# Grouped-query attention: another PSUM split, another place for the division, and orders written out

## The chip, the cores and the metric

The kernel runs on one core of one Trainium2 chip. A core has a matrix engine (TensorE, PE in the profile), a vector engine (VectorE, DVE), an activation engine (ScalarE, ACT), a general engine (GpSimd, POOL), and SyncE (SP), which only issues transfers here. Each engine works through its own list of instructions in order and waits on semaphores for the others. Matmul results land in PSUM, eight banks of 2 KB per partition; everything else lives in SBUF. The metric is the device time of one execution in microseconds, lower is better.

## The reference

Eight batches, 512 positions, 32 query heads, 8 key/value heads, head size 64, all float32. Four query heads share a key/value head.

```python
scores = np.einsum('bhqd,bhkd->bhqk', Q, K_expanded) * scale      # scale = 1/sqrt(64)
weights = np.exp(scores - np.max(scores, axis=-1, keepdims=True))
weights = weights / (np.sum(weights, axis=-1, keepdims=True) + 1e-10)
output = np.einsum('bhqk,bhkd->bhqd', weights, V_expanded)
```

## The kernel before

The work is cut into 32 units: a batch and two neighbouring key/value heads, so 8 query heads. A unit has 4 pairs of query heads (`p` counts pairs, 128 in all, called slots below). A pair has 4 chunks of 128 keys (`kc`).

For one chunk `emit_scores_chunk` makes two matmuls (L169), one for each head `m`. Each uses 64 rows of the array (the head size), head 0 on partitions 0 to 63 and head 1 on 64 to 127, and writes 512 float32 columns, so the chunk's tile `s_unit` fills two PSUM banks with 128 keys by 2x512 queries. The exponential moves it to SBUF as bf16 (`pt`): three chunks in four by ScalarE's Exp (L186), the second one (`kc` = 1) by VectorE (L177), which computes bits of a bf16 number with one multiply and add. Nothing subtracts the maximum.

`emit_pv_chunk` multiplies `pt` by V (L206): 8 matmuls a chunk, 65 columns each, since V carries a column of ones that sums the weights. A pair's output is 8 blocks (2 heads by 4 query tiles `qc`) of 65 columns, and 4 matmuls, one a chunk, add up to a block: 128 of them a unit. `emit_norm` takes the reciprocal of the ones column (L223) and multiplies (L224) on VectorE, straight from PSUM, for each pair.

Q and K come in with positions on partitions, and PE turns them with `ident` (L118 for K, L130 for Q), 24 transposes a unit in three groups of 8, each copied out by VectorE (L120, L134). K is loaded twice into `k_nat`, so that each head's keys stand on both halves of the partitions.

PSUM: a ring of three two-bank tiles, `spsum_pool`, shared by scores and transposes, and one two-bank tile for the output (`pv_pool`). All loads and stores are issued by GpSimd, loads converting float32 to bf16: of a unit's eight loads six move rows of one head (64 numbers) and two, for Q, rows of 256, and a store moves rows of 512. The order of work on each engine is made by the framework's scheduler from the program's order.

Of the kernel before, what the change touches and what calls it, by code (L numbers as in the profile page):

```python
# [12 lines left out]
U16 = mybir.dt.uint16  # L14


@with_exitstack
def kernel(
# [7 lines left out]
    nc = tc.nc  # L26
# [7 lines left out]
    NPAIR = HPG // 2  # L34
    NSLOT = NU * 2 * NPAIR

    scale = 1.0 / math.sqrt(D)

    DVE_KC = 1

    SCHRAUD_C = 5.0
    LOAD_PREFETCH = 2
    STORE_DELAY = 2

    A_schr = (2.0 ** 7) / math.log(2.0) * scale
    B_schr = 127.0 * (2.0 ** 7) - SCHRAUD_C

    const_pool = ctx.enter_context(tc.tile_pool(name="const", bufs=1))
    qnat_pool = ctx.enter_context(tc.tile_pool(name="qnat", bufs=LOAD_PREFETCH + 2))
    knat_pool = ctx.enter_context(tc.tile_pool(name="knat", bufs=LOAD_PREFETCH + 2))  # L50
    v_pool = ctx.enter_context(tc.tile_pool(name="v", bufs=LOAD_PREFETCH + 2))
    qt_pool = ctx.enter_context(tc.tile_pool(name="qt", bufs=6))
    kt_pool = ctx.enter_context(tc.tile_pool(name="kt", bufs=3))
    pt_pool = ctx.enter_context(tc.tile_pool(name="pt", bufs=3))
    osb_pool = ctx.enter_context(tc.tile_pool(name="osb", bufs=STORE_DELAY + 2))
    misc_pool = ctx.enter_context(tc.tile_pool(name="misc", bufs=8))

    spsum_pool = ctx.enter_context(tc.tile_pool(name="spsum", bufs=3, space=bass.MemoryType.PSUM))
    pv_pool = ctx.enter_context(tc.tile_pool(name="pv", bufs=1, space=bass.MemoryType.PSUM))

    ident = const_pool.tile([128, 128], BF16)
    make_identity(nc, ident)

    def unit_bgp(u):
        return u // GP, u % GP

    loads = {}

    def emit_load_q(u):
        b, gp = unit_bgp(u)  # L70
        g0 = 2 * gp
        h_base = g0 * HPG
        q_nat = qnat_pool.tile([128, SC, 2, HPG, D], BF16, name="q_nat")
        for g in range(2):
            nc.gpsimd.dma_start(  # L75
                out=q_nat[:, :, g, :, :],
                in_=Q[b, :, h_base + g * HPG:h_base + (g + 1) * HPG, :].rearrange(
                    "(sc p) h d -> p sc h d", p=128
                ),
            )  # L80
        loads.setdefault(u, {})["q"] = q_nat

    def emit_load_k(u):
        b, gp = unit_bgp(u)
        g0 = 2 * gp
        k_nat = knat_pool.tile([128, SC, 2, 2, D], BF16, name="k_nat")
        for g in range(2):
            for c in range(2):
                nc.gpsimd.dma_start(  # L89
                    out=k_nat[:, :, g, c, :],  # L90
                    in_=K[b, :, g0 + g, :].rearrange("(sc p) d -> p sc d", p=128),
                )
        loads.setdefault(u, {})["k"] = k_nat

    def emit_load_v(u):
        b, gp = unit_bgp(u)
        g0 = 2 * gp
        v_tile = v_pool.tile([128, SC, 2, D + 1], BF16, name="v")
        nc.gpsimd.memset(v_tile[:, :, :, D:D + 1], 1.0)  # L99
        for g in range(2):  # L100
            nc.gpsimd.dma_start(  # L101
                out=v_tile[:, :, g, 0:D],
                in_=V[b, :, g0 + g, :].rearrange("(sc p) d -> p sc d", p=128),
            )
        loads.setdefault(u, {})["v"] = v_tile

    LOAD_BATCHES = (emit_load_q, emit_load_k, emit_load_v)

    trans = {}

    def emit_trans_kt(u):
        k_nat = loads[u]["k"]
        kt_ps = spsum_pool.tile([128, 2, S], FP32, name="s_unit")[:, 0, :].bitcast(
            BF16
        ).rearrange("p (g sc c) -> p g sc c", g=2, sc=SC)
        for g in range(2):
            for sc in range(SC):
                nc.tensor.transpose(kt_ps[:, g, sc, :], k_nat[:, sc, g, :, :], ident)  # L118
        kt_tile = kt_pool.tile([128, 2, S], BF16, name="kt")
        nc.vector.tensor_copy(out=kt_tile, in_=kt_ps)  # L120
        trans.setdefault(u, {})["kt"] = kt_tile

    def emit_trans_qt(u, g):
        q_nat = loads[u]["q"]
        qt_ps = spsum_pool.tile([128, 2, S], FP32, name="s_unit")[:, 0, :].bitcast(
            BF16
        ).rearrange("p (i sc c) -> p i sc c", i=NPAIR, sc=SC)
        for i in range(NPAIR):
            for sc in range(SC):
                nc.tensor.transpose(  # L130
                    qt_ps[:, i, sc, :], q_nat[:, sc, g, 2 * i:2 * i + 2, :], ident
                )
        qt_tile = qt_pool.tile([128, NPAIR, S], BF16, name="qt")
        nc.vector.tensor_copy(out=qt_tile, in_=qt_ps)  # L134
        trans.setdefault(u, {}).setdefault("qt", {})[g] = qt_tile

    TRANS_BATCHES = (
        emit_trans_kt,
        lambda u: emit_trans_qt(u, 0),
        lambda u: emit_trans_qt(u, 1),  # L140
    )

    pending_stores = {}

    def emit_store(u, split=False):
        b, gp = unit_bgp(u)
        h_base = 2 * gp * HPG
        o_sb = pending_stores.pop(u)
        nc.gpsimd.dma_start(  # L149
            out=out[b, :, h_base:h_base + 2 * HPG, :].rearrange(  # L150
                "(sc p) h d -> p sc h d", p=128
            ),
            in_=o_sb,
        )

    jobs = {}
    osb = {}

    def emit_scores_chunk(p, kc):
        st = jobs[p]  # L160
        u, g, i = st["u"], st["g"], st["i"]
        kt_all = trans[u]["kt"]
        qt_tile = trans[u]["qt"][g]
        pt_tile = st["pt"]
        pair_idx = st["pidx"]

        s_unit = spsum_pool.tile([128, 2, S], FP32, name="s_unit")
        for m in range(2):
            nc.tensor.matmul(  # L169
                s_unit[:, m, :],  # L170
                kt_all[64 * m:64 * m + 64, g, kc * 128:(kc + 1) * 128],
                qt_tile[64 * m:64 * m + 64, i, :],
                start=True,
                stop=True,
            )
        if kc == DVE_KC:
            nc.vector.tensor_scalar(  # L177
                out=pt_tile[:, kc, :, :].bitcast(U16),
                in0=s_unit[:, :, :],
                scalar1=float(A_schr),  # L180
                scalar2=float(B_schr),
                op0=mybir.AluOpType.mult,
                op1=mybir.AluOpType.add,
            )
        else:
            nc.scalar.activation(  # L186
                out=pt_tile[:, kc, :, :],
                in_=s_unit[:, :, :],
                func=mybir.ActivationFunctionType.Exp,
                scale=float(scale),  # L190
            )

    def emit_pv_chunk(p, kc):
        st = jobs[p]
        u, g = st["u"], st["g"]
        v_tile = loads[u]["v"]
        pt_tile = st["pt"]
        if kc == 0:
            pv_tile = pv_pool.tile([128, 2, 512], FP32, name="pv").rearrange(
                "p m (qc c) -> p m qc c", qc=SC  # L200
            )
            st["opsums"] = pv_tile[:, :, :, 0:D + 1]
        o_psums = st["opsums"]
        for qc in range(SC):
            for m in range(2):
                nc.tensor.matmul(  # L206
                    o_psums[:, m, qc, :],
                    pt_tile[:, kc, m, qc * 128:(qc + 1) * 128],
                    v_tile[:, kc, g, :],
                    start=(kc == 0 and qc == 0),  # L210
                    stop=(kc == SC - 1 and qc == SC - 1),
                )

    def emit_norm(p):
        st = jobs.pop(p)
        u, g, i = st["u"], st["g"], st["i"]
        if u not in osb:
            osb[u] = osb_pool.tile([128, SC, 2, NPAIR, 2, D], FP32, name="o_sb")
            pending_stores[u] = osb[u]
        o_sb = osb[u]  # L220
        o_psums = st["opsums"]
        inv = misc_pool.tile([128, 2, SC], FP32, name="inv")
        nc.vector.reciprocal(out=inv, in_=o_psums[:, :, :, D:D + 1])  # L223
        nc.vector.tensor_tensor(  # L224
            out=o_sb[:, :, g, i, :, :].rearrange("p qc m d -> p m qc d"),
            in0=o_psums[:, :, :, 0:D],
            in1=inv[:, :, :, None].to_broadcast((128, 2, SC, D)),
            op=mybir.AluOpType.mult,
        )
        if st["pidx"] == 2 * NPAIR - 1:  # L230
            osb.pop(u)
# [5 lines left out]
    for fn in TRANS_BATCHES:  # L237
        fn(0)
# [70 lines left out]
```

## Time and profile before

| what | value |
|---|---|
| median of 3 runs (lowest, highest) | 451.97 us (451.85, 452.49) |
| profiled execution, first to last instruction | 449.0 us |
| PE matmuls, busy | 371.9 us (83%) |
| VectorE, busy | 326.0 us (73%) |
| ScalarE, busy | 367.0 us (82%) |
| GpSimd, busy | 219.0 us (49%) |
| transfer engines, queue of GpSimd | 95.7% of 16 engines' span |
| bytes read from and written to memory | 58.72 MB, 33.55 MB |

The profile gives no time of its own for the profiled execution beside its span of 449.0 us; the median of the timed runs lies 3.0 us above that span. Busy time counts instructions from start to end, and matmuls overlap each other, so a busy PE can still take more. PEld is PE loading weights, one load ahead of every matmul. In rows of groups the number after the bar is the sum in us, then the mean in ns.

### The profile page before, as it was taken

To read this page: it belongs to the slowest core of one execution; us is meant where nothing else is said; L and a number is where in the kernel's file an instruction comes from. 1 tells how busy PE (TensorE), PEld (TensorE's weight loads), DVE (VectorE), ACT (ScalarE), POOL (GpSimd) and SP (SyncE) were. 2 spreads that over 40 slices of the span, in tenths; PEclk is the share of its full clock that TensorE was granted. 3 is DMA by queue.
4 is the path that set the end of the run, shared out by engine and by line. 5 is a ranking of instruction groups with operands and counts; after the bars stand their busy time and mean duration, and the time that the engine had idled before them with its cause. 6 is when DMAs were issued, how large, how long until landed. Compare 5 with 4: busy or idle time off the path is not lost.

```text
span 449.0 us, 13535 instructions
## 1 busy us (share of the span) xinstructions
PE 371.9 (83%) x5888; PEld 219.5 (49%) x5888; DVE 326.0 (73%) x480; ACT 367.0 (82%) x385; POOL 219.0 (49%) x326
## 2 busy tenths in 40 slices
PE   2888888888888888888888888888888888888882
PEld 1445545555455455455554554554545545545541
DVE  1577787777787777778777778777778777777761
ACT  1688888888888888888888888888888888888881
POOL 9988556454456554446645445645445652200000
PEclk9999999999999999999999999999999999999998
DMA  9999999999999999999999999999999999212222
GB/s 90 151 160 213 206 173 148 159 126 121 168 173 147 156 140 113 160 176 149 158 154 110 145 172 165 148 156 128 122 169 172 147 155 157 36 80 96 95 95 93
DMA packets 143930, 63.78 MB, mean 142 GB/s; under 512 B 102912, under 2 KB 135680, under 8 KB 143872
## 3 DMA queue, kind: packets, MB, share of 16 engines
q0 software_dynamic: 143872, 62.93, 95.7%
q8 instruction: 46, 0.75, 0.7%
q14 instruction: 12, 0.10, 0.1%
HBM read 58.72 MB, written 33.55 MB: 206 GB/s over the span
## 4 chain that ended last, share of the span: by engine, by line
PE 65%; issue 13%; ACT 11%; POOL 7%; DMA 1%; ACTq 1%; DVE 0%; POOLq 0%
PE s_unit L169 30%; PE pv L206 28%; ACT pt L186 11%; PE s_unit L130 5%; POOL k_nat L89 3%; PE s_unit L118 3%; POOL q_nat L75 2%; POOL v L101 1%; DMA q_nat<-in_Q_dram 1%; POOL out_dram L149 1%; ACTq L186 1%; DVE pt L177 0%; POOLq L304 0%; POOL v L99 0%; POOL ident masks.py:199 0%
## 5 line engine op out<-in xcount | busy, mean ns | idle before, releaser
L186 ACT ACTIVATE pt<-s_unit 128x1024 bf16<-128x1024 f32 x384 | 365.7, 1024 | 72.5 <-PE s_unit L169 72.5
L169 PE MATMUL s_unit<-qt,kt 64*128 64x512 bf16 x1024 | 191.0, 385 | 60.0 <-ACT pt L186 58.2
L206 PEld LDWEIGHTS <-pt 128*128 128x128 bf16 x4096 | 139.2, 98 | 114.9 <-issue 75.8
L206 PE MATMUL pv<-v,pt 128*128 128x65 bf16 x4096 | 170.3, 195 | 1.0 <-DVE o_sb L224 1.0
L177 DVE TENSOR_SCALAR pt<-s_unit 128x1024 uint16<-128x1024 f32 x128 | 156.3, 1221 | 16.1 <-PE s_unit L169 11.3
L89 POOL DMA_DIRECT2D k_nat<-in_K_dram x128 | 96.7, 783 | 1.2 <-issue 1.1
L224 DVE TENSOR_TENSOR o_sb<-pv,inv 128x512 f32<-128x512 f32 x128 | 88.5, 691 | 4.5
L169 PEld LDWEIGHTS <-kt 64*128 64x128 bf16 x1024 | 40.9, 94 | 97.1 <-issue 78.7
L223 DVE RECIPROCAL inv<-pv 128x8 f32<-128x8 f32 x128 | 26.6, 208 | 83.8 <-PE pv L206 83.8
L75 POOL DMA_DIRECT2D q_nat<-in_Q_dram x64 | 48.2, 766 | 47.1 <-PE s_unit L130 44.9
L99 POOL MEMSET v<- 128x8 bf16 x32 | 4.9, 152 | 122.6 <-PE pv L206 122.6
L101 POOL DMA_DIRECT2D v<-in_V_dram x64 | 47.9, 759 | 4.0 <-DMA q_nat<-in_Q_dram 0.7
L149 POOL DMA_DIRECT2D out_dram<-o_sb x32 | 24.9, 779 | 48.6 <-DVE o_sb L224 48.6
L134 DVE COPY qt<-s_unit 128x1024 bf16<-128x1024 bf16 x64 | 43.5, 679 | 2.4 <-PE s_unit L130 2.4
L130 PE MATMUL s_unit<-ident,q_nat 128*128 128x128 bf16 x512 | 39.9, 222 | 1.8 <-DMA q_nat<-in_Q_dram 1.7
L130 PEld LDWEIGHTS <-q_nat 128*128 128x128 bf16 x512 | 30.3, 99 | 2.4 <-DMA q_nat<-in_Q_dram 2.2
L120 DVE COPY kt<-s_unit 128x1024 bf16<-128x1024 bf16 x32 | 21.8, 680 | 9.5 <-PE s_unit L118 9.5
L118 PE MATMUL s_unit<-ident,k_nat 128*128 128x128 bf16 x256 | 20.5, 225 | 6.6 <-DMA k_nat<-in_K_dram 6.6
L118 PEld LDWEIGHTS <-k_nat 128*128 128x128 bf16 x256 | 15.4, 100 | 7.2 <-issue 5.7
L186 ACT ACT_TABLE_LOAD x1 | 1.3, 1283 | 0.7 <-PEq L293 0.7
masks.py:199 POOL TENSOR_SCALAR_AFFINE_SELECT ident<-ident 128x128 bf16<-128x128 bf16 x1 | 0.3, 305 | 0.1
masks.py:197 POOL MEMSET ident<- 128x128 bf16 x1 | 0.2, 205 | 0.3 <-POOLq L293 0.3
(4 smaller groups left out, 0.4 us busy)
## 6 DMA issues: line engine op xcount, KB each, us to landing
out_dram<-o_sb POOLq DMA_DIRECT2D x32, 1024.0 KB, 5.3
q_nat<-in_Q_dram POOLq DMA_DIRECT2D x64, 256.0 KB, 5.2
k_nat<-in_K_dram POOLq DMA_DIRECT2D x128, 64.0 KB, 4.9
v<-in_V_dram POOLq DMA_DIRECT2D x64, 64.0 KB, 3.1
```

The costliest lines, as they stand in the source:

```text
L75: nc.gpsimd.dma_start(out=q_nat[:, :, g, :, :], in_=Q[b, :, h_base + g * HPG:h_base + (g + 1) * HPG, :].rearrange("(sc p) h d -> p sc h d" ...
L89: nc.gpsimd.dma_start(out=k_nat[:, :, g, c, :], in_=K[b, :, g0 + g, :].rearrange("(sc p) d -> p sc d", p=128),)
L101: nc.gpsimd.dma_start(out=v_tile[:, :, g, 0:D], in_=V[b, :, g0 + g, :].rearrange("(sc p) d -> p sc d", p=128),)
L118: nc.tensor.transpose(kt_ps[:, g, sc, :], k_nat[:, sc, g, :, :], ident)
L130: nc.tensor.transpose(qt_ps[:, i, sc, :], q_nat[:, sc, g, 2 * i:2 * i + 2, :], ident)
L134: nc.vector.tensor_copy(out=qt_tile, in_=qt_ps)
L149: nc.gpsimd.dma_start(out=out[b, :, h_base:h_base + 2 * HPG, :].rearrange("(sc p) h d -> p sc h d", p=128), in_=o_sb,)
L169: nc.tensor.matmul(s_unit[:, m, :], kt_all[64 * m:64 * m + 64, g, kc * 128:(kc + 1) * 128], qt_tile[64 * m:64 * m + 64, i, :], start=True, ...
L177: nc.vector.tensor_scalar(out=pt_tile[:, kc, :, :].bitcast(U16), in0=s_unit[:, :, :], scalar1=float(A_schr), scalar2=float(B_schr), op0=my ...
L186: nc.scalar.activation(out=pt_tile[:, kc, :, :], in_=s_unit[:, :, :], func=mybir.ActivationFunctionType.Exp, scale=float(scale),)
L206: nc.tensor.matmul(o_psums[:, m, qc, :], pt_tile[:, kc, m, qc * 128:(qc + 1) * 128], v_tile[:, kc, g, :], start=(kc == 0 and qc == 0), sto ...
L224: nc.vector.tensor_tensor(out=o_sb[:, :, g, i, :, :].rearrange("p qc m d -> p m qc d"), in0=o_psums[:, :, :, 0:D], in1=inv[:, :, :, None]. ...
```

## The change

The units, the pairs, the chunks, the score matmuls and the split of the exponential between ScalarE and VectorE stay (the VectorE one has another additive constant). What differs:

- PSUM: a ring of three two-bank tiles for scores alone (`spsum`), and a ring of two one-bank tiles (`xpsum`) that transposes and outputs share.
- Outputs are made block by block: 4 matmuls in a row add up to one block. Blocks are gathered in groups of 7, 7, 7, 4 and 7 to a bank. VectorE copies a group as it is (`raw`), and once a unit takes the reciprocal of 32 sums (L212). GpSimd does the division for the whole unit (L214).
- K is turned once (4 transposes a unit, so 20 in all); two transfers on SyncE's queue make a copy with the halves exchanged (`kx`), and the head whose half is wrong reads that one.
- Loads: one for Q a unit, one for K and one for V a batch, rows of 512 numbers in all of them (1 KB in bf16). GpSimd spreads V to leave room for the ones column (`spread_v`).
- The order on all engines is the program's. After each chunk's scores a loop puts in filler (blocks of output, transposes) for 0.33 us by its own costs, if the next filler is ready by a lag of two chunks after its pair.

```diff
+    DVE_KC = 1
+    qn_pool = ctx.enter_context(tc.tile_pool(name="qn", bufs=PREF))   # PREF = 4
...
+    pt_pool = ctx.enter_context(tc.tile_pool(name="pt", bufs=4))
+    raw_pool = ctx.enter_context(tc.tile_pool(name="raw", bufs=3))
+    osb_pool = ctx.enter_context(tc.tile_pool(name="osb", bufs=3))
...
+    spsum = ctx.enter_context(tc.tile_pool(name="spsum", bufs=3, space=bass.MemoryType.PSUM))
+    xpsum = ctx.enter_context(tc.tile_pool(name="xpsum", bufs=2, space=bass.MemoryType.PSUM))
...
+    def load_q(u):
+        b, gp = divmod(u, GP)
+        t = qn_pool.tile([128, SC, HU * D], BF16, name="q_nat")
+        nc.gpsimd.dma_start(
+            out=t,
+            in_=Q[b, :, HU * gp:HU * (gp + 1), :].rearrange(
+                "(sc p) h d -> p sc (h d)", p=128
+            ),
+        )
...
+    def spread_v(b):
+        t = v1_pool.tile([128, SC, KV, D + 1], BF16, name="v1")
+        nc.gpsimd.memset(t[:, :, :, D:D + 1], 1.0)
+        nc.gpsimd.tensor_copy(
+            out=t[:, :, :, 0:D],
+            in_=vn.pop(b).rearrange("p sc (h d) -> p sc h d", h=KV),
+        )
...
             nc.tensor.matmul(
-                s_unit[:, m, :],
-                kt_all[64 * m:64 * m + 64, g, kc * 128:(kc + 1) * 128],
-                qt_tile[64 * m:64 * m + 64, i, :],
+                s[:, m, :],
+                kt[u][0 if m == g else 1][64 * m:64 * m + 64, kc * 128:(kc + 1) * 128],
+                qt[u][64 * m:64 * m + 64, i, :],
...
+    class Outputs:
...
+        def ready(self, step, lag):
+            pair = self.u * HPG + (self.first + self.at) // BLK
+            return step >= SC * (pair + 1) + lag
+        def emit(self):
...
+                self.o = xpsum.tile([128, 2048], mybir.dt.uint8, name="x").bitcast(FP32)
...
+            for kc in range(SC):
+                nc.tensor.matmul(
+                    self.o[:, self.at * (D + 1):(self.at + 1) * (D + 1)],
+                    pt[:, kc, m, qc * 128:(qc + 1) * 128],
+                    v1[u // GP][:, kc, 2 * (u % GP) + 2 * i // HPG, :],
+                    start=(self.at == 0 and kc == 0),
+                    stop=(self.at == self.n - 1 and kc == SC - 1),
+                    skip_group_check=True,
+                )
...
+            nc.vector.tensor_copy(
+                out=raws[u][:, self.first:self.first + self.n, :],
+                in_=self.o[:, 0:self.n * (D + 1)],
+            )
+            if self.first + self.n == HPG * BLK:
+                finish(u)
...
+    class Turn:
...
+            nc.tensor.transpose(self.x[:, self.at * 128:(self.at + 1) * 128], src, ident)
...
+                nc.vector.tensor_copy(out=k, in_=self.x[:, 0:S])
+                x = kt_pool.tile([128, S], BF16, name="kx")
+                nc.sync.dma_start(out=x[64:128], in_=k[0:64])
+                nc.sync.dma_start(out=x[0:64], in_=k[64:128])
...
+    def finish(u):
...
+        nc.vector.reciprocal(out=inv, in_=raw[:, :, D])
+        o = osb_pool.tile([128, SC, HU, D], FP32, name="o_sb")
+        nc.gpsimd.tensor_tensor(
+            out=o.rearrange("p qc h d -> p h qc d"),
...
+    COST = {Outputs: 0.122, Turn: 0.056}
+    QUOTA = 0.33
+    LAG = 2
+    def unit_fill(u):
+        yield Outputs(u, 0, 7)
+        yield Outputs(u, 7, 7)
+        if u + 2 < NU:
+            yield Turn(u + 2, 0)
+            yield Turn(u + 2, 1)
+        yield Outputs(u, 14, 7)
+        if u + 2 < NU:
+            yield Turn(u + 2, None)
+        yield Outputs(u, 21, 4)
+        yield Outputs(u, 25, 7)
+    with tc.manual_schedule(engines={PE, ACT, DVE, POOL, SP}):
+        load_k(0)
+        load_q(0)
+        load_q(1)
+        load_v(0)
+        load_q(2)
+        load_q(3)
+        spread_v(0)
+        for t in (Turn(0, None), Turn(0, 0)):
+            while not t.emit():
+                pass
+        fill = [Turn(0, 1), Turn(1, None), Turn(1, 0), Turn(1, 1)]
+        for u in range(NU):
+            fill.extend(unit_fill(u))
...
+                scores(p, kc)
+                budget += QUOTA
+                while budget > 0 and fill and fill[0].ready(step, LAG):
+                    f = fill[0]
+                    budget -= COST[type(f)]
+                    if f.emit():
+                        fill.pop(0)
...
+                budget = min(budget, 2 * QUOTA)
```

How the instructions stand now, at three places. On PE, in the middle of the kernel before, two chunks of scores stand together (tiles 2271 and 2275) between the last K transpose and the first output matmul of a run of 16:

```order
L118 MATMUL s_unit_2253<-ident_88,k_nat_1746 128x128
L169 LDWEIGHTS kt_2003
L169 MATMUL s_unit_2271<-qt_2074,kt_2003 128x512
L169 LDWEIGHTS kt_2003
L169 MATMUL s_unit_2271<-qt_2074,kt_2003 128x512
L169 LDWEIGHTS kt_2003
L169 MATMUL s_unit_2275<-qt_2074,kt_2003 128x512
L169 LDWEIGHTS kt_2003
L169 MATMUL s_unit_2275<-qt_2074,kt_2003 128x512
L206 LDWEIGHTS pt_2200
L206 MATMUL pv_2279<-v_1558,pt_2200 128x65
```

On PE in the changed kernel, around the K transposes of a unit (L189 is any transpose, L108 a score, L149 an output, `x` the one-bank tile):

```order
L189 LDWEIGHTS k_nat_101
L189 MATMUL x_611<-ident_94,k_nat_101 128x128
L108 LDWEIGHTS kt_372
L108 MATMUL s_616<-qt_301,kt_372 128x512
L108 LDWEIGHTS kx_374
L108 MATMUL s_616<-qt_301,kx_374 128x512
L189 LDWEIGHTS k_nat_101
L189 MATMUL x_611<-ident_94,k_nat_101 128x128
L149 LDWEIGHTS pt_495
L149 MATMUL x_626<-v1_113,pt_495 128x65
```

One chunk now stands alone between fillers. Over a unit in the steady part, PE's 16 chunks stand in 10 runs: 1, 2, 1, 3, 4 and five times 1 chunk, and the runs of 3 and 4 stand before and behind the longest filler, 32 output matmuls. Before, a unit had 8 runs of 2 chunks.

On VectorE before, for one unit (L120 and L134 copy transposes, L177 is its share of the exponential):

```order
L120 COPY kt<-s_unit 128x1024
L177 TENSOR_SCALAR pt<-s_unit 128x1024
L223 RECIPROCAL inv<-pv 128x8
L224 TENSOR_TENSOR o_sb<-pv,inv 128x2x4x64
L134 COPY qt<-s_unit 128x1024
L177 TENSOR_SCALAR pt<-s_unit 128x1024
L223 RECIPROCAL inv<-pv 128x8
L224 TENSOR_TENSOR o_sb<-pv,inv 128x2x4x64
```

VectorE now, one unit (L162 copies raw outputs):

```order
L117 TENSOR_SCALAR pt<-s 128x1024
L162 COPY raw<-x 128x455
L117 TENSOR_SCALAR pt<-s 128x1024
L162 COPY raw<-x 128x455
L203 COPY qt<-x 128x1024 x2
L117 TENSOR_SCALAR pt<-s 128x1024
L162 COPY raw<-x 128x455
L195 COPY kt<-x 128x512
L117 TENSOR_SCALAR pt<-s 128x1024
L162 COPY raw<-x 128x260
L162 COPY raw<-x 128x455
L212 RECIPROCAL inv<-raw 128x32
```

Four reciprocals and four multiplications of a unit have become five copies and one reciprocal, and three copies of transposes are still there, one of them half as wide. On GpSimd, before, about a unit:

```order
L101 DMA v<-in_V_dram 128x4x64 x2
L89 DMA k_nat<-in_K_dram 128x4x64
L149 DMA out_dram<-o_sb 128x4x512
L89 DMA k_nat<-in_K_dram 128x4x64 x3
L75 DMA q_nat<-in_Q_dram 128x4x256 x2
L99 MEMSET v 128x8
```

GpSimd now, two units, one of them with the next batch's V spread in it (L97):

```order
L72 DMA q_nat<-in_Q_dram 128x4x512
L214 TENSOR_TENSOR o_sb<-raw,inv 128x8x4x64
L222 DMA out_dram<-o_sb 128x4x512
L96 MEMSET v_990 128x32
L97 COPY v_990<-v_nat 128x32x64
L72 DMA q_nat<-in_Q_dram 128x4x512
L214 TENSOR_TENSOR o_sb<-raw,inv 128x8x4x64
L222 DMA out_dram<-o_sb 128x4x512
```

Eight loads a unit have become one and a half, and a multiplication over 2048 numbers a partition stands ahead of every store.

More of the change, by code (lines that the diff above doesn't have):

```diff
@@ L14 @@
 U16 = mybir.dt.uint16
+PE = mybir.EngineType.PE
+ACT = mybir.EngineType.Activation
+DVE = mybir.EngineType.DVE
+POOL = mybir.EngineType.Pool
+SP = mybir.EngineType.SP
 @with_exitstack
@@ L83, in emit_load_k @@
[L83 to L135, printed above, removed]
@@ L152, in emit_store, with load_k @@
             ),
-            in_=o_sb,
         )
[L156 to L167, printed above, removed]
+        qn[u] = t
+    def load_k(b):
+        t = kn_pool.tile([128, SC, KV * D], BF16, name="k_nat")
+        nc.gpsimd.dma_start(
+            out=t, in_=K[b].rearrange("(sc p) h d -> p sc (h d)", p=128)
+        )
+        kn[b] = t
@@ L186, in emit_scores_chunk @@
             nc.scalar.activation(
[L187 to L188 removed]
+                out=pt[:, kc, :, :],
+                in_=s,
                 func=mybir.ActivationFunctionType.Exp,
@@ L191, in emit_scores_chunk @@
             )
[L193 to L200, printed above, removed]
-            )
[L202 to L211, printed above, removed]
-                )
```

206 lines of the change are left out of this document (100 added, 106 removed).

## The prediction

> **What bounds the kernel now.** First the page's header, for shares:
>
> ```profile
> span 449.0 us, 13535 instructions
> PE 371.9 (83%) x5888; PEld 219.5 (49%) x5888; DVE 326.0 (73%) x480; ACT 367.0 (82%) x385; POOL 219.0 (49%) x326
> ...
> q0 software_dynamic: 143872, 62.93, 95.7%
> ```
>
> No engine is full; the transfer engines nearly are. Two windows tell whether they set the pace (columns: length, then PE, PEld, DVE, ACT, POOL busy with counts, clock, DMA share, GB/s):
>
> ```profile
> 200.00:300.00 100.00, 85.94 (x1382) 51.00 (x1382) 76.03 (x113) 85.63 (x91) 51.96 (x77) 1.00 1.01 145
> 400.00:435.00 35.00, 29.87 (x468) 17.04 (x467) 25.63 (x38) 29.79 (x33) 2.27 (x3) 1.00 0.23 92
> ```
>
> After 400 us nothing is loaded and the share falls from 1.01 to 0.23, yet ScalarE is busy 29.79/35.00 = 85.1% against 85.6%. So transfers do not set the pace, and neither the longer rows nor GpSimd's freed time are worth anything in the steady part. What does is a loop. The chain of waits, one slot:
>
> ```profile
> 203.55 0.39 PE s_unit L169 x2
> 203.94 0.59 PE pv L206 x16
> 204.53 0.54 PE s_unit L169 x4
> 205.07 0.59 PE pv L206 x16
> 205.66 0.45 PE s_unit L130 x8
> 206.10 0.34 PE s_unit L169 x2
> 206.44 0.03 ACTq L186
> 206.47 0.37 ACT pt L186
> 206.84 0.04 issue
> 206.89 0.37 PE s_unit L169
> ```
>
> From 203.55 to 206.89 is 3.34 us, times 128 slots 427 us: the whole kernel but its ends. In it PE waits for ScalarE to free a score tile, and ScalarE waits for PE:
>
> ```profile
> 204.90 2.85 ACT L186 ACTIVATE pt<-s_unit 128x1024 bf16<-128x1024 f32 x3 [0.48 <-PE s_unit L169]
> 208.23 1.02 ACT L186 ACTIVATE pt<-s_unit 128x1024 bf16<-128x1024 f32 x1 [0.48 <-PE s_unit L169]
> ```
>
> One exponential takes 1.02 us, each further one (2.85 - 1.02)/2 = 0.915. ScalarE stands 0.48 us a slot because the next slot's third chunk is behind 16 output matmuls. So neither engine is the bound alone: three tiles, shared with transposes, in runs of two chunks and 16 matmuls.
>
> **The change, part by part.** Prices of PE work come from starts of its weight loads in that slot (start, length):
>
> ```profile
> 203.55 0.09 PEld L169 LDWEIGHTS <-kt 64*128 64x128 bf16 x1 [0.73 <-issue]
> 203.87 0.54 PEld L206 LDWEIGHTS <-pt 128*128 128x128 bf16 x16 [0.23 <-issue]
> 204.46 0.12 PEld L169 LDWEIGHTS <-kt 64*128 64x128 bf16 x4
> 205.00 0.53 PEld L206 LDWEIGHTS <-pt 128*128 128x128 bf16 x16 [0.42 <-issue]
> 205.47 0.46 PEld L130 LDWEIGHTS <-q_nat 128*128 128x128 bf16 x8
> 206.03 0.11 PEld L169 LDWEIGHTS <-kt 64*128 64x128 bf16 x3
> ```
>
> One chunk of scores and the turn to output matmuls take 203.87 - 203.55 = 0.32, two take 205.00 - 204.46 = 0.54: a chunk is 0.22, the turn 0.10. 16 output matmuls before transposes take 0.47 (0.0295 each), before scores 204.46 - 203.87 = 0.59: turning back costs 0.12. Eight transposes with that turn take 0.56: 0.055 each.
>
> Scores use half the array's rows for each head, outputs and transposes all of them. The Trainium skill (TensorEngine Tiling (Array Packing), Key Properties) says that changing the tiling mode drains the engine, with no price. The trace agrees: 0.10 and 0.12 at each turn. The rule speaks against this change, which turns more often; were turns free, the sum would come down to the ScalarE floor below, near 382.
>
> *PE, one unit.* 16 chunks x 0.22 = 3.52; 10 runs x 0.22 for both turns = 2.20 (8 before); 128 output matmuls x 0.0295 = 3.78; 20 transposes x 0.055 = 1.10 (four fewer). Sum 10.60. Four output matmuls now add to the same 65 columns in a row, where before eight others lay between; no row shows that order. It cannot be quicker than 0.0295, since the count of columns is the same; the slowest neighbour is a transpose, 0.055. I take 0.0295, because weights change at each matmul either way.
>
> *The score ring.* A tile comes free 0.39 (pair) + 0.03 + 1.02 + 0.04 = 1.48 us after its scores start, if ScalarE is idle. In the run of 4 chunks PE reaches the last after 0.66 and waits 0.82. The last of the run of 3 needs the tile of the single chunk ahead of it, 12 output matmuls earlier: 0.22 + 0.10 + 0.35 + 0.12 + 0.44 = 1.23, wait 0.25. Elsewhere fillers cover 1.48. Together 1.07 a unit. Transposes no longer take score tiles.
>
> *VectorE and the two-bank ring.* Its rows:
>
> ```profile
> L177 DVE TENSOR_SCALAR pt<-s_unit 128x1024 uint16<-128x1024 f32 x128 | 156.3, 1221 | 16.1 <-PE s_unit L169 11.3
> ...
> L224 DVE TENSOR_TENSOR o_sb<-pv,inv 128x512 f32<-128x512 f32 x128 | 88.5, 691 | 4.5
> ...
> L223 DVE RECIPROCAL inv<-pv 128x8 f32<-128x8 f32 x128 | 26.6, 208 | 83.8 <-PE pv L206 83.8
> ...
> L134 DVE COPY qt<-s_unit 128x1024 bf16<-128x1024 bf16 x64 | 43.5, 679 | 2.4 <-PE s_unit L130 2.4
> ```
>
> Twice the float32 numbers from PSUM cost 1221 - 691 = 530 ns, so 1.04 ns each: a raw copy of 455 takes 0.63, of 260 0.43, the reciprocal of 32 0.23, the narrower K copy about 0.42 (half of L134 less its fixed part). A unit: 4 x 1.22 + 4 x 0.63 + 0.43 + 2 x 0.68 + 0.42 + 0.23 = 9.84 us, against 4 x (1.22 + 0.69 + 0.21) + 3 x 0.68 = 10.52. It fits under PE, but in order: a copy behind an exponential comes up to 1.2 us late. A group of 7 blocks gives PE 0.83 us of work and two or more chunks around it, which covers that. The K group is short: 4 transposes and a chunk, 0.22 + 0.44 = 0.66, while the copy of the group before, whose bank comes next, needs 0.14 + 0.63 + 0.04 = 0.81: a wait of 0.15 to 0.20. If it found an exponential started, 1.2 more.
>
> So a unit is 10.60 + 1.07 + 0.20 = 11.9 us, against 13.34. Floor from ScalarE: 12 x 0.915 = 10.98. 32 x 11.9 = 381; the last two units have no transposes (20 x 0.055 and some turns each), less 3: 378.
>
> *GpSimd.* Loads fall from 8 to 1.5 a unit, 0.77 each; added are a 2048-wide multiplication a unit and a 2048-wide copy a batch. Rows nearest:
>
> ```profile
> L75 POOL DMA_DIRECT2D q_nat<-in_Q_dram x64 | 48.2, 766 | 47.1 <-PE s_unit L130 44.9 <-PE s_unit L169 1.2 <-issue 1.0
> ...
> L99 POOL MEMSET v<- 128x8 bf16 x32 | 4.9, 152 | 122.6 <-PE pv L206 122.6
> masks.py:199 POOL TENSOR_SCALAR_AFFINE_SELECT ident<-ident 128x128 bf16<-128x128 bf16 x1 | 0.3, 305 | 0.1
> ```
>
> 120 more elements cost 153 ns, 1.28 ns each: 2.7 us for 2048 with one input, 5.4 if two inputs cost double. VectorE's 1.04 ns gives 2.3 as the lower end. I take 4. With 1.5 loads and a store (1.9 us) and a quarter of the copy (1), GpSimd works 7 of 11.9 us: hidden, since `raw` has three buffers. It shows once, at the end. The Trainium skill (GPSIMD Engine Reference, Performance versus the Vector engine) states 4497 ns for a float32 `tensor_tensor` of 2048; by it the end would be 0.5 later. No row here shows one.
>
> *SyncE.* Two copies of K halves a unit, needed two units later: hidden, with over 20 us of cover; the first unit's lie beside the first Q load.
>
> *The start.*
>
> ```profile
> 7.16 0.58 PE L118 MATMUL s_unit<-ident,k_nat 128*128 128x128 bf16 x4 [1.30 <-DMA k_nat<-in_K_dram]
> ...
> 10.49 1.03 PE L130 MATMUL s_unit<-ident,q_nat 128*128 128x128 bf16 x8 [0.27 <-DMA q_nat<-in_Q_dram]
> 11.46 0.60 PE L169 MATMUL s_unit<-qt,kt 64*128 64x512 bf16 x2
> ```
>
> and the window behind it, columns as above:
>
> ```profile
> 8.00:22.00 14.00, 11.40 (x118) 6.53 (x119) 7.63 (x10) 7.35 (x8) 14.00 (x22) 1.00 1.71 156
> ```
>
> Six fewer issues precede Q, but K brings all four units' heads and its exchanged copy must land. I keep 11.5 for the first scores (9.5 to 14). V is fourth in the queue: 4 x 0.52 MB at 156 GB/s is 13.4 us from about 3; longer rows should be quicker. I take 13 for landing and 4 for spreading: 17. Outputs are due at the seventh chunk, 11.5 + 6 x 0.74 = 16. I charge 2 (0 to 6), since PE, in order, waits for V there.
>
> *The end.*
>
> ```profile
> 437.83 0.60 PE L169 MATMUL s_unit<-qt,kt 64*128 64x512 bf16 x3
> ...
> 441.50 0.69 DVE L224 TENSOR_TENSOR o_sb<-pv,inv 128x512 f32<-128x512 f32 x1
> 442.49 0.75 POOL L149 DMA_DIRECT2D out_dram<-o_sb  x1 [11.37 <-DVE o_sb L224]
> ```
>
> 449.0 - 437.8 = 11.2 from the last scores; raw copy and reciprocal replace 0.90 by 0.86, and the multiplication adds 4: 15.
>
> **Sum.** 11.5 + 2 + 378 + 15 = 406.5 of span. The median of the runs before is 451.97, 3.0 above the span; so 409.5, taken as 409. About 0.2% is what timings of this kernel can tell from no change.
>
> **Rivals.**
> 1. *ScalarE becomes the bound*: weight loads slip ahead and turns cost less when chunks stand apart. 32 x 10.98 = 351; 351 + 11.5 + 1.5 + 15 + 3 = 382. For it: only 0.92 us a unit separates it. Against: the turns are in every slot.
> 2. *VectorE's fixed order is late*: each unit one copy finds an exponential just started and holds a bank or score tile 1 us longer: 32 us, 441. Half of that, or V landing late, gives 420 to 430. For it: 1.2 us operations and a ring of two. Against: 2 us a unit idle.
> 3. *Slower: adding to the same columns.* If a matmul must wait for its forerunner's sum, 128 a unit grow from 0.0295. At the transposes' 0.055, PE gets 3.3 us more, 15.2 a unit, 515 in all. It decides from a unit of (452 - 31.5)/32 = 13.1, which is 0.0395 a matmul. Against: PE already streams outputs and transposes with nothing between.
> 4. *GpSimd holds the loads.* Its multiplication would have to take over 10 us, twice the upper bound.
>
> **Chances.** Forecast (398 to 420) 0.57; rival 1 (378 to 398) 0.14; rival 2 (420 to 446) 0.18; rivals 3 and 4 (above 453) 0.09; within 0.2% 0.02. Faster 0.89, same 0.02, slower 0.09. For 8 in 10 the range takes the forecast, the nearer half of rival 1 and most of rival 2: 392 to 436.
>
> **What would show it.** ScalarE busy near 90%; a unit 11.9 us; in each unit L108 waits about 0.8 us for ScalarE behind the run of 32 output matmuls; L149 still 0.03 apart; transfer share under half; L214 near 4 us. Wrong if L149 is 0.04 apart, if PE waits on L162 often, or if V comes after 20 us.

## The result, and the profile after

The changed kernel takes 417.23 us (median of 4 runs, 416.41 to 417.69), against 451.91 us for the kernel before in the same session. The ratio is 0.9237 (95% interval 0.9218 to 0.9257), 34.7 us less. The forecast was 409 us, its range 392 to 436.

The page's header after, as for the kernel before:

```profile
span 414.6 us, 12965 instructions
PE 360.6 (87%) x5760; PEld 226.4 (55%) x5760; DVE 308.6 (74%) x416; ACT 370.4 (89%) x385; POOL 193.5 (47%) x134
q0 software_dynamic: 34048, 58.73, 63.4%
```

VectorE and GpSimd are busy a little less than before, PE makes 128 transposes fewer, and ScalarE does the same work in a shorter time. The transfer queue of GpSimd has a quarter of the packets. A window of the steady part (length, then PE, PEld, DVE, ACT, POOL busy, clock, DMA share, GB/s):

```profile
200.00:300.00 100.00, 92.42 (x1493) 58.13 (x1490) 80.47 (x110) 95.92 (x101) 50.47 (x33) 1.00 0.73 163
```

ScalarE was busy 85.6% of the same window before. The chain of waits for one unit, from one ring wait to the next like it:

```profile
203.82 0.39 PE s L108 x2
204.22 0.83 PE x L149 x24
205.05 0.28 PE x L189 x5
205.32 0.32 PE s L108 x2
...
208.78 0.24 PE x L149 x4
...
209.04 0.64 DVE raw L162
...
209.73 0.53 PE x L149 x12
210.26 0.56 PE s L108 x4
...
210.84 1.02 ACT pt L126
...
211.88 1.03 ACT pt L126
...
212.96 0.39 PE s L108 x2
213.35 1.08 PE x L149 x32
214.43 0.34 PE s L108 x2
...
214.79 1.03 ACT pt L126
...
215.87 0.39 PE s L108 x2
```

From 203.82 to 215.87 a unit takes 12.05 us; before it was 13.34. PE is on the chain for 8.1 of these 12.05 us. The three places where it is not are the three that the forecast named: the copy of the third group of blocks (L162 at 209.04) that frees a bank of the two, and ScalarE before the last chunk of the run of three (212.96) and of the run of four (215.87).

The whole difference in span is 449.0 - 414.6 = 34.4 us. The unit gives 32 x 1.29 = 41.3. The end takes back 3.1: it is 414.6 - 400.28 = 14.3 us from the last scores, 11.2 before. About 4 are left, and they fall to the start.

### The profile page after: what moved, and what is told of

It is laid out like the page before. It is cut to its first block, busy times and chain, and to the rows that moved or that the text cites. A ratio compares the mean times of both kernels' runs of the same rounds, so it can differ in the third digit from the quotient of the medians.

```text
span 414.6 us, 12965 instructions
## 1 busy us (share of the span) xinstructions
PE 360.6 (87%) x5760; PEld 226.4 (55%) x5760; DVE 308.6 (74%) x416; ACT 370.4 (89%) x385; POOL 193.5 (47%) x134
## 4 chain that ended last, share of the span: by engine, by line
PE 62%; ACT 23%; DVE 5%; issue 4%; DMA 3%; POOL 2%; POOLq 0%
PE x L149 28%; PE s L108 25%; ACT pt L126 23%; PE x L189 9%; DVE raw L162 5%; POOL o_sb L214 2%; DMA k_nat<-in_K_dram 1%; DMA kx<-kt 1%; DVE pt L117 0%; POOLq L313 0%; POOL out_dram L222 0%; DVE qt L203 0%; DVE kt L195 0%; DVE inv L212 0%; POOL ident masks.py:197 0%
## 5 line engine op out<-in xcount | busy, mean ns | idle before, releaser
L126 ACT ACTIVATE pt<-s 128x1024 bf16<-128x1024 f32 x384 | 369.2, 1023 | 30.6 <-PE s L108 23.1
L214 POOL TENSOR_TENSOR o_sb<-raw,inv 128x2048 f32<-128x2048 f32 x32 | 115.7, 3615 | 193.1 <-DVE inv L212 193.1
L108 PE MATMUL s<-qt,kx 64*128 64x512 bf16 x512 | 175.8, 385 | 24.1 <-ACT pt L126 22.8
L108 PE MATMUL s<-qt,kt 64*128 64x512 bf16 x512 | 176.2, 385 | 5.3 <-ACT pt L126 1.4
L149 PEld LDWEIGHTS <-pt 128*128 128x128 bf16 x4096 | 144.3, 97 | 63.1 <-issue 60.0
L117 DVE TENSOR_SCALAR pt<-s 128x1024 uint16<-128x1024 f32 x128 | 154.4, 1207 | 30.5 <-PE s L108 30.5
L162 DVE COPY raw<-x 128x455 f32<-128x455 f32 (+1 forms) x160 | 94.3, 589 | 37.5 <-PE x L149 34.4
L108 PEld LDWEIGHTS <-kt 64*128 64x128 bf16 x512 | 42.4, 93 | 52.5 <-issue 33.9
L203 DVE COPY qt<-x 128x1024 bf16<-128x1024 bf16 x64 | 44.2, 691 | 17.8 <-PE x L189 17.8
L108 PEld LDWEIGHTS <-kx 64*128 64x128 bf16 x512 | 40.1, 93 | 28.1 <-issue 13.7
L189 PE MATMUL x<-ident,q_nat 128*128 128x128 bf16 x512 | 46.8, 225 | 2.5 <-DMA q_nat<-in_Q_dram 1.9
L189 PEld LDWEIGHTS <-q_nat 128*128 128x128 bf16 x512 | 30.6, 100 | 18.5 <-issue 16.3
L189 PE MATMUL x<-ident,k_nat 128*128 128x128 bf16 x128 | 18.1, 227 | 7.3 <-DMA k_nat<-in_K_dram 7.3
L149 PE MATMUL x<-v_113,pt 128*128 128x65 bf16 x512 | 21.9, 194 | 0.3
L149 PE MATMUL x<-v_3951,pt 128*128 128x65 bf16 x512 | 21.7, 194 | 0.3
L149 PE MATMUL x<-v_990,pt 128*128 128x65 bf16 x512 | 21.7, 194 | 0.3
L149 PE MATMUL x<-v_5925,pt 128*128 128x65 bf16 x512 | 21.7, 194 | 0.3
L149 PE MATMUL x<-v_4938,pt 128*128 128x65 bf16 x512 | 21.7, 194 | 0.3
L149 PE MATMUL x<-v_2964,pt 128*128 128x65 bf16 x512 | 21.7, 194 | 0.3
L149 PE MATMUL x<-v_1977,pt 128*128 128x65 bf16 x512 | 21.7, 194 | 0.3
```

The lines of the kernel that those rows point to most:

```text
L108: nc.tensor.matmul(s[:, m, :], kt[u][0 if m == g else 1][64 * m:64 * m + 64, kc * 128:(kc + 1) * 128], qt[u][64 * m:64 * m + 64, i, :], st ...
L117: nc.vector.tensor_scalar(out=pt[:, kc, :, :].bitcast(U16), in0=s, scalar1=float(A_schr), scalar2=float(B_schr), op0=mybir.AluOpType.mult, ...
L126: nc.scalar.activation(out=pt[:, kc, :, :], in_=s, func=mybir.ActivationFunctionType.Exp, scale=float(scale),)
L149: nc.tensor.matmul(self.o[:, self.at * (D + 1):(self.at + 1) * (D + 1)], pt[:, kc, m, qc * 128:(qc + 1) * 128], v1[u // GP][:, kc, 2 * (u ...
L162: nc.vector.tensor_copy(out=raws[u][:, self.first:self.first + self.n, :], in_=self.o[:, 0:self.n * (D + 1)],)
L189: nc.tensor.transpose(self.x[:, self.at * 128:(self.at + 1) * 128], src, ident)
```

## Experiments

All are edits of the changed kernel, but one of the kernel before. Each time is a median, and the ratio is to the kernel before on the same chip (449.6 to 452.5 us in all of them).

### The rows of the loads

```diff
-        nc.gpsimd.dma_start(
-            out=t, in_=K[b].rearrange("(sc p) h d -> p sc (h d)", p=128)
-        )
+        for h in range(KV):
+            nc.gpsimd.dma_start(
+                out=t[:, :, h * D:(h + 1) * D],
+                in_=K[b, :, h, :].rearrange("(sc p) d -> p sc d", p=128),
+            )
...  (V the same way, Q in two loads a unit)
```

> The changed kernel, but with loads in the row lengths of before: Q in two loads a unit (rows of 256 numbers), K and V in one load a head (rows of 64). Six loads a unit instead of 1.5. Theory (transfers and GpSimd's loads are hidden in the steady part): unit stays 12.05 us; GpSimd has 4.5 loads x 0.77 = 3.5 us more, 9.5 of 12.05, still hidden; the start may be 1 to 3 us later, so 416 to 421 us. Rival (the longer rows made the gain, transfers set the pace before): 430 us or more, with the transfer share back near 1.

Measured: 419.02 us, ratio 0.9287 (0.9269 to 0.9305). The steady part in the same window, and the start:

```profile
200.00:300.00 100.00, 93.02 (x1502) 58.46 (x1502) 80.18 (x110) 95.89 (x101) 79.19 (x71) 1.00 1.02 166
```

```profile
14.95 0.61 PE L113 MATMUL s<-qt,kx 64*128 64x512 bf16 x1
```

The transfer share is back at 1.02 and GpSimd is busy 79% instead of 50%, yet ScalarE is busy 95.9% as with long rows. Only the first scores come later, at 14.95 instead of 13.41, and the total grows by 1.8. The long rows are worth that and no more.

### The division on VectorE

```diff
-        nc.gpsimd.tensor_tensor(
+        nc.vector.tensor_tensor(
```

> The changed kernel, but the unit's multiplication runs on VectorE instead of GpSimd (2048 float32 from SBUF, about 2.3 us by VectorE's 1.04 ns a number). Theory (VectorE has only 2 us a unit to spare and works in order): 10.0 + 2.3 = 12.3 us of work a unit, and the exponential behind the multiplication is up to 2.3 us late and holds a score tile, so a unit of 12.9 to 13.4, 445 to 460 us in all. Rival (where the division runs does not matter, VectorE's idle time takes it): 415 to 420 us, as the end is also shorter by 1.3.

Measured: 462.46 us, ratio 1.0252 (1.0227 to 1.0276): slower than the kernel before, and 2 us above the theory's range. The chain of waits at the end of a unit:

```profile
208.25 0.64 DVE raw L162
...
209.30 0.04 DVE o_sb L214
209.34 2.17 issue
211.51 0.69 DVE pt L117
```

The multiplication (2.29 us, starting at 209.30) now stands between a copy and an exponential for which PE waits. From one multiplication to the next a unit takes 13.25 us (209.30 to 222.55), as the theory had it, but eight of the units take 14.45 (194.85 to 209.30), each with a stretch of 3.4 us in which the granted clock is 0.50 (the last section shows one). These eight are 9.6 us of the time; without them it would lie inside the theory's range. Giving the multiplication to GpSimd is a condition of the rest, though VectorE was idle a quarter of the time. This is not quite the form before, which multiplied a pair at a time straight from PSUM.

### Transposes in the score ring

```diff
-                self.x = xpsum.tile([128, 2048], mybir.dt.uint8, name="x").bitcast(BF16)
+                self.x = spsum.tile([128, 2, S], FP32, name="s")[:, 0, :].bitcast(BF16)
```

> The changed kernel, but transposes write into tiles of the score ring of three, as before; outputs keep the two one-bank tiles. Theory (transposes out of the score ring are part of the gain): three more tiles a unit pass through the ring, each held from its first transpose to the end of VectorE's copy, so PE waits 0.3 to 0.6 us more a unit: 12.4 to 12.6, 427 to 435 us. Rival (the split of PSUM does nothing, fillers cover it): 415 to 419 us.

Measured: 435.48 us, ratio 0.9655 (0.9634 to 0.9676): half of the gain is gone. A unit takes 12.58 us (201.78 to the like place at 214.36), 0.53 more. In the chain the new wait is a score chunk behind VectorE's copy of transposes:

```profile
203.60 0.29 PE s L189 x3
...
203.91 0.70 DVE qt L203
...
204.65 0.41 PE s L108 x2
```

### One shape of the array

```diff
-                s[:, m, :],
-                kt[u][0 if m == g else 1][64 * m:64 * m + 64, kc * 128:(kc + 1) * 128],
-                qt[u][64 * m:64 * m + 64, i, :],
+                s[:, m, 0:256],
+                kt[u][0][:, kc * 128:(kc + 1) * 128],
+                qt[u][:, i, 256 * m:256 * (m + 1)],
...
+        twice = s[:, :, None, 0:256].to_broadcast((128, 2, 2, 256))
```

> The changed kernel, but a chunk's two score matmuls use all 128 rows of the array with 256 columns each (a sum over both heads, half the queries), and the exponentials read each half twice. PE's score time stays 0.215 us a chunk, ScalarE's and VectorE's work too, but scores, outputs and transposes now have one shape of array. Theory (the 0.10 and 0.12 us at each turn come from the change of the array's shape): turns vanish, 10 x 0.22 = 2.2 us a unit; ScalarE's floor of 11.0 becomes the bound: unit 11.0 to 11.3, 382 to 395 us, weight loads of outputs 0.22 behind those of scores instead of 0.32. Rival (the turn is a cost of changing the operands, whatever the shape): 414 to 418 us.

Measured: 382.94 us, ratio 0.8477 (0.8447 to 0.8507), 34 us under the changed kernel. The chain of waits:

```profile
205.51 3.21 ACT pt L127 x4
...
208.75 0.38 PE s L108 x2
209.13 0.72 PE x L150 x24
209.85 0.28 PE x L190 x5
210.13 0.22 PE s L108 x2
```

The same 24 output matmuls and 5 transposes, then a chunk: 0.72, 0.28 and 0.22, where the changed kernel shows 0.83, 0.28 and 0.32. Both turns are gone, and most of the chain is ScalarE; the like wait comes again at 219.75, a unit of 11.0, which is the floor of 12 x 0.915. So a turn costs about 0.1 us each way because the array's shape changes, and it is on the path. The Trainium skill (TensorEngine Tiling (Array Packing), Key Properties) says that such a change drains the engine. The run agrees with it, but does not show that it is a drain and not some other cost of the change. The kernel of this run leaves out half of the queries; it measures the turns and is no candidate. Scores also no longer wait for `kx` here, which is worth up to 2 us at the start.

### The order alone, on the kernel before

```diff
+    with tc.manual_schedule(engines={PE, ACT, DVE, POOL, SP}):
         for u in range(min(LOAD_PREFETCH + 1, NU)):
...  (all loops as they were, indented)
```

> The kernel before, unchanged but for the order: all engines keep the program's order and the score ring's tiles are given out in turn, instead of the scheduler's order and choice. Theory (before, PE waited each slot until ScalarE had finished the fourth chunk of the slot ahead, because that chunk's tile came next): given out in turn, a slot without transposes no longer meets that tile and takes about 2.9 us, one with them 2.9 to 3.5; a unit 12.7 instead of 13.34, so 426 to 436 us. Rival (the scheduler's order is as good, all the gain is in the new split of PSUM and the new parts): 448 to 454 us.

Measured: 435.19 us, ratio 0.9643 (0.9619 to 0.9666), 16.4 us under its neighbour of 451.59. In a slot without transposes PE no longer waits for the last exponential of the slot ahead, as the kernel before does until 213.57. Only the fourth chunk waits, until 208.13, for the first exponential of its own slot:

```profile
206.00 0.34 PE s_unit L174 x2
206.36 1.72 ACT pt L191 x2
...
208.13 0.39 PE s_unit L174 x2
```

The unit, read from 200.53 to the like place at 213.38, is 12.85 us. PE's list of work is nearly the same in both; whose end a chunk waits for is not, and by the edit that is the tile that it is given. No instruction's duration shows that, only the chain.

### Filler spread

```diff
+        if u + 2 < NU:
+            yield Turn(u + 2, 0)
         yield Outputs(u, 0, 7)
-        yield Outputs(u, 7, 7)
         if u + 2 < NU:
-            yield Turn(u + 2, 0)
             yield Turn(u + 2, 1)
+        yield Outputs(u, 7, 7)
         yield Outputs(u, 14, 7)
...
-                budget = min(budget, 2 * QUOTA)
+                budget = min(budget, 0.45)
```

> The changed kernel with the filler in another order: a unit's first and second transposes stand ahead of its first and second group of blocks, and the budget carries at most 0.45 us instead of 0.66, so no filler is longer than 28 output matmuls and runs of 3 and 4 chunks without filler mostly go. Theory (the two ring waits of 0.84 and 0.27 us a unit come from the filler of 32 matmuls and the runs of 3 and 4 chunks around it): the waits fall by 0.6 to 0.8 us a unit, to a unit of 11.2 to 11.4, 390 to 397 us. Rival (the waits only move, as ScalarE is 96% busy already): 411 to 418 us.

Measured: 398.30 us, ratio 0.8821 (0.8800 to 0.8842), 19 us under the changed kernel and 1.3 above the expected range. The unit is 11.36. The window of the steady part:

```profile
200.00:300.00 100.00, 97.52 (x1597) 61.91 (x1598) 84.07 (x116) 99.42 (x107) 53.19 (x35) 1.00 0.77 174
```

ScalarE is busy 99.4%, and yet a unit is 0.38 us above ScalarE's floor of 10.98: 12 exponentials take 0.947 each. Busy time counts an exponential from start to end, 1.02 us, while two in a row follow each other at 0.915, so a share near 100% can still hide exponentials that start late. The chain of waits shows what is left:

```profile
244.32 0.56 PE s L108 x4
...
244.98 1.23 DVE pt L117
246.20 0.57 DVE raw L162
...
246.81 0.53 PE x L149 x12
```

A copy of outputs stands behind VectorE's exponential, and the next outputs wait for its bank. That is rival 2 of the prediction, on a small scale. That this wait alone accounts for the 0.38 is not shown.

### Fewer turns

```diff
         yield Outputs(u, 0, 7)
-        yield Outputs(u, 7, 7)
         if u + 2 < NU:
             yield Turn(u + 2, 0)
+        yield Outputs(u, 7, 7)
+        if u + 2 < NU:
             yield Turn(u + 2, 1)
         yield Outputs(u, 14, 7)
...
-    QUOTA = 0.33
+    QUOTA = 0.5
...
-                budget = min(budget, 2 * QUOTA)
+                budget = min(budget, 0.33)
```

> The changed kernel with longer fillers in fewer places: quota 0.5 us with at most 0.33 carried over, and transposes between the groups of blocks; 8 runs of scores a unit instead of 10. Theory (a unit is 10.60 us of PE work at 10 turns plus ring waits): two turns fewer save 0.44, the waits stay near 0.8 + 0.3, so a unit of 11.3 to 11.7, 391 to 405 us. Rival (only the number of the waits counts): 410 to 418 us.

Measured: 401.30 us, ratio 0.8892 (0.8870 to 0.8915), a unit of 11.61. That is 0.44 less, the price of two turns by the forecast's figures. The order of the filler changed as well, and with it PE's waits (in one unit it stands 0.51 us for ScalarE and 0.37 for a copy of L162), so the agreement is no proof. Fewer turns and shorter waits do about the same.

### The start, twice

```diff
         load_v(0)
-        load_q(2)
-        load_q(3)
         spread_v(0)
+        load_q(2)
+        load_q(3)
```

> The changed kernel, but the Q loads of the third and fourth unit are issued behind the spreading of V, so they do not run beside the first K copy (kx). Theory (kx came at 13.4 us instead of 11.5 because its transfers shared the engines with five loads in flight): first full chunk at 12 to 13 us, 0.5 to 1.5 us less in all, 415.5 to 416.8. Rival (kx's 4 us are its own latency): 417.0 to 417.6.

Measured: 417.14 us, ratio 0.9240 (0.9218 to 0.9262): no change. `kx` comes at 13.57:

```profile
13.57 0.61 PE L108 MATMUL s<-qt,kx 64*128 64x512 bf16 x1 [1.54 <-DMA kx<-kt]
```

The edit did not empty the transfer engines: their share from 8 to 14 us is 1.23 in both kernels, since the second Q and V are still in flight. So this run cannot tell the theory from the rival, but the trace of the changed kernel can. The same two transfers, in the window 8:15 and in 366:372, where no load is left (the last number is the time from issue to landing):

```profile
kx<-kt SPq DMA_DIRECT2D x2, 64.0 KB, 5.3
...
kx<-kt SPq DMA_DIRECT2D x2, 64.0 KB, 2.0
```

With the engines nearly idle the copy takes 2.0 us, so most of the 5 us at the start comes from the loads beside it, as the theory had it.

```diff
+                if u == 0:
+                    y = xpsum.tile([128, 2048], mybir.dt.uint8, name="x").bitcast(BF16)
+                    for sc in range(SC):
+                        nc.tensor.transpose(
+                            y[:, sc * 128:(sc + 1) * 128], k0x[:, sc, :], ident
+                        )
+                    nc.vector.tensor_copy(out=x, in_=y[:, 0:S])
...
+        for h in range(2):
+            nc.gpsimd.dma_start(
+                out=k0x[:, :, (1 - h) * D:(2 - h) * D],
+                in_=K[0, :, h, :].rearrange("(sc p) d -> p sc d", p=128),
+            )
```

> The changed kernel, but the first unit's exchanged K does not go through the two transfers on SyncE's queue: its two heads are loaded once more with the halves exchanged, behind the first Q, and turned on PE. Theory (the start is 2 us late because kx takes 4 us and comes at 13.4): first full chunk at 11.6 to 12.6, 0.8 to 1.8 us less, 415.4 to 416.4. Rival (PE's slow start or the second Q load set it): 416.9 to 417.6.

Measured: 415.19 us, ratio 0.9191 (0.9168 to 0.9213), 2.0 us less. The first full chunk starts at 12.65 instead of 13.41, and now waits for Q's copy; the place that is at 23.34 in the changed kernel comes at 22.58. So the start gives 0.8. The two profiled spans differ by 1.8, and 0.8 of that lies at the other end: from the last scores it is 412.9 - 399.38 = 13.5 us instead of 14.3. The last store is issued sooner after the multiplication, in the changed kernel and here:

```profile
408.58 0.79 POOL L222 DMA_DIRECT2D out_dram<-o_sb  x1 [0.96 <-POOL o_sb L214]
...
407.01 0.79 POOL L230 DMA_DIRECT2D out_dram<-o_sb  x1 [0.30 <-POOL o_sb L222]
```

In the changed kernel's other units in the window from 200 to 300 us that gap is 0.30 too. Why this edit shortens the last one is not shown. The theory named the start alone, and that it came near the forecast total is in part luck.

### The end, twice

```diff
+        parts = ((nc.gpsimd, 0, HU),)
+        if u == NU - 1:
+            parts = ((nc.gpsimd, 0, 3), (nc.vector, 3, HU))
```

> The changed kernel, but for the last unit alone the multiplication is split: 3 of 8 heads on GpSimd, 5 of 8 on VectorE. Theory (the two work side by side): the last 3.6 us become about 1.5, 2.1 less, 415.1 us. Rival (Trainium skill, SBUF — State Buffer, Who interferes with whom: a VectorE instruction with two SBUF inputs and a GpSimd instruction that reads SBUF exclude each other): one after the other, 1.4 + 1.4 us, 0.8 less, 416.4 us. If the end is not on the path: 417.2.

Measured: 416.14 us, ratio 0.9220 (0.9197 to 0.9243), 1.1 less: near the rival. The last lines of the timeline:

```profile
404.03 1.49 DVE L218 TENSOR_TENSOR o_sb<-raw,inv 128x1280 f32<-128x1280 f32 x1
404.09 2.76 POOL L218 TENSOR_TENSOR o_sb<-raw,inv 128x768 f32<-128x768 f32 x1 [6.54 <-DVE inv L212]
```

3 of 8 heads alone would be 3.6 x 3/8 = 1.4 us on GpSimd. It takes 2.76, and about 1.3 of that lie behind the end of VectorE's 1.49. The Trainium skill's rule (SBUF — State Buffer, Who interferes with whom) fits: a VectorE instruction with two SBUF inputs and a reading GpSimd instruction go one after the other. The 1.4 is an estimate; the 3 heads were not run on GpSimd alone.

```diff
+        nc.gpsimd.tensor_tensor(
+            out=o.rearrange("p qc h d -> p h qc d"),
...  (the same multiplication once more)
```

> The changed kernel, but GpSimd makes each unit's multiplication twice over. Theory (GpSimd's division is hidden but for the last unit): 9.7 us of GpSimd work in a unit of 12.05 stay hidden, only the end grows by one more multiplication: 417.2 + 3.6 = 420.8 us, 420 to 422. Rival (GpSimd is near the path, through the raw ring or its loads and stores): 425 us or more.

Measured: 420.67 us, ratio 0.9318 (0.9297 to 0.9339), 3.4 more.

```profile
200.00:300.00 100.00, 93.07 (x1515) 58.87 (x1512) 80.76 (x110) 95.97 (x100) 78.37 (x41) 1.00 0.76 169
```

GpSimd is busy 78% instead of 50% and ScalarE's share is the same. The division is hidden in the steady part, and it shows at the end.

### Together

Filler spread, split end and exchanged first K in one kernel:

> The filler order of the spread run, the split multiplication of the last unit and the first unit's K loaded exchanged, all together. Theory (three separate places on the path, so the gains add): 398.3 - 1.1 - 1.3 = 396, 395 to 397.5 us. Rival (the start's gain is eaten by the next wait there): 397 to 398.5.

Measured: 395.52 us, ratio 0.8755 (0.8732 to 0.8777). It is the fastest of these kernels that compute the whole output, and the total adds up as expected. Of the 2.4 us between the profiled spans of this run and of the filler spread alone (396.4 and 394.0), 1.7 lie behind the last scores (14.3 and 12.6), where the shorter gap before the last store shows again (0.30 instead of 0.96).

## Why the prediction was right, point by point

*The bound before.* The forecast took transfers for hidden and the loop of PE and ScalarE through three score tiles for the bound. The short rows (+1.8 us, the steady window unchanged) show the first, and the order alone (-16.4) shows that the loop could be shortened with no work removed. The median came out 8 us above the forecast, inside the range.

*PE's sum.* 10.60 us a unit was nearly right: 12.05 less the three waits below, 1.35 together, is 10.70. 32 output matmuls take from 201.24 to 202.31 with the turn back, 0.0297 each, not 0.0295. They add to the same columns in a row, four at a time, at full speed, so rival 3 is out. The turns cost 0.10 and 0.12 as priced, and the run with one shape shows that the array's shape is their cause. It took 382.9 us, where the forecast put the kernel with free turns near 382.

*The ring waits.* Forecast 0.82 and 0.25, measured 0.84 (the run of four starts at 202.32, its last chunk at 203.82, less three chunks of 0.22) and 0.27 (212.96 instead of 212.69); a tile is free 1.50 us after its scores start, not 1.48. The wait for a bank behind the K transposes was forecast as 0.15 to 0.20 and is 0.24. Spreading the filler takes 0.7 us off a unit, so these waits make up most of the 1.07 that separate the kernel from ScalarE's floor.

*The unit.* 11.9 forecast, 12.05 measured: about 0.1 from these waits and rates, the rest unassigned. Over 32 units this is 5 us of the 8 by which the forecast was low.

*The start.* This term was mis-sized. It was 11.5 for the first scores and 2 for V. V was not late (L97, L149 below):

```profile
15.30 1.89 POOL L97 COPY v_113<-v_nat 128x2048 bf16<-128x2048 bf16 x1 [8.78 <-DMA v_nat<-in_V_dram]
...
17.23 0.80 PE L189 MATMUL x<-ident,q_nat 128*128 128x128 bf16 x6 [0.63 <-DVE qt L203]
...
20.87 1.02 PE L149 MATMUL x<-v_113,pt 128*128 128x65 bf16 x28
```

Its spreading ends at 17.2, before the first outputs. The exchanged K was late, which the forecast had called hidden beside the first Q:

```profile
8.36 5.00 DMA kx<-kt
...
13.41 0.60 PE s L108
14.02 0.76 PE x L189 x6
```

So the first full chunk starts at 13.41, just where 11.5 + 2 put it, but for another reason: that agreement is luck. Behind it a chunk takes PE 0.60 instead of 0.39 and six transposes 0.76 instead of 0.45, up to 20 us, at a granted clock of 1.00; why is not shown. The forecast's own rows of the start had it (eight transposes in 1.03 us at 10.49, a chunk in 0.60 at 11.46), and it put no price on it. In a steady unit the ring wait ends 6.76 us after the first chunk (209.11 to 215.87). Behind 13.5 that is 20.3; it came at 23.34, 3.1 us later. An estimate from the rows: five chunks at 0.21 more and 28 transposes at 0.05 more are 2.5 us, and PE stands 0.63 for a copy that VectorE makes behind an exponential (17.23 above). The rest about cancels.

*GpSimd and the end.* 4 us taken, 3.6 measured (the last row of L214); 15 us for the end, 14.3 measured.

```profile
L214 POOL TENSOR_TENSOR o_sb<-raw,inv 128x2048 f32<-128x2048 f32 x32 | 115.7, 3615 | 193.1 <-DVE inv L212 193.1
```

The bounds, 2.3 from VectorE and 5.4 from small GpSimd instructions, held it; the 4497 ns that the Trainium skill (GPSIMD Engine Reference, Performance versus the Vector engine) states for this count of numbers is 0.9 above the 3615 ns measured, and the measurement decides.

*VectorE.* Copies of 455 took 0.632 and of 260 0.420 as worked out; the reciprocal of 32 numbers took 0.353, not 0.23. It reads SBUF where the one before read PSUM; what makes it longer is not shown. Rival 2 did not come in the steady part: PE waits for L162 once a unit.

*The list of signs.* One was wrong: the transfer share is 0.73, not under half. It changes nothing in the sum.

## What to carry to other kernels

When two engines pass tiles around a small ring, write down one period as a sum of PE's pieces and find which tile's release each piece needs; here the waits came out within 0.1 us, and the order of filler between the score chunks was worth as much as the ring split (19 and 18 us). An engine's idle share does not say that it can take more work: VectorE had a quarter of its time free and a 2.3 us instruction in its queue still cost 45 us, some 10 of them at half the granted clock, because exponentials stood behind it. Nor does a busy share near 100% say that an engine is at its floor. Price the turn between matmuls of different array shapes from the starts of weight loads, and count turns.

## What the runs showed of the hardware

GpSimd's multiplication and VectorE's did not run side by side: 2.76 us for an estimated 1.4 us of work. Beside VectorE's exponentials and copies, which read PSUM, GpSimd's full multiplication takes 3.62 us (at 201.41), as long as at the end, where VectorE has nothing to do (3.61 at 404.01). In the run with the division on VectorE the granted clock fell to half for some stretches (windows, columns as above):

```profile
195.00:200.00 5.00, 3.64 (x62) 2.48 (x59) 4.95 (x4) 4.14 (x5) 2.56 (x4) 0.87 0.25 97
200.00:201.00 1.00, 1.00 (x10) 0.51 (x7) 0.63 (x1) 0.00 (x0) 0.42 (x1) 0.50 1.02 324
```

PE had been busy 3.64 of 5 us and was then granted 0.50 at full load, which stretched six transposes from 0.45 to 0.75 us. The unit after it, with the same wait of PE, kept 1.00. There are eight such stretches of 3.4 us, one in each of the units of 14.45 us, and they bring the mean clock to 0.961 against 0.990 in the changed kernel. What sets them off is not shown.
